# A decoder layer on one core: filler steps with later due times, and another order in the input projection

## The chip, the cores and the metric

The kernel runs on one core of a Trainium2 chip. The metric is the time of one execution on the device, in microseconds (us); lower is better. Five engines work side by side, each through its own list of instructions in order: PE (TensorE, matmuls), DVE (VectorE), ACT (ScalarE), POOL (GpSimd) and SP (SyncE, which here only starts transfers). POOL also starts transfers. PE writes its results to eight banks of PSUM, each [128, 512] in float32.

## The reference

One layer on x of [2048, 1024] in float32: a mixer and an MLP, each between two RMS norms, with residual sums.

```python
h = rms_norm(x, mix_norm_pre)
z = h @ w_in                      # [2048, 2560]: q, k, v (512 each), xr, gr (512 each)
q, k, v, xr, gr = split(z)
attn = dilated_attention(q, k, v) # 8 heads of 64; three windows (128, 1), (512, 4), (2048, 16), mixed
                                  # by their softmax denominators
xr = causal_depthwise_conv(xr)    # 4 taps
rec = rg_lru(xr) * gelu(gr)       # gated linear recurrence along the sequence
x = x + rms_norm(concat(attn, rec) @ w_out, mix_norm_post)
h = rms_norm(x, mlp_norm_pre)
x = x + rms_norm(relu(h @ w_ff_in) ** 2 @ w_ff_out, mlp_norm_post)
```

## The kernel before

**Numbers.** Each float32 operand of a large matmul is split in a high and a low part (`split`, L54: ACT writes the high part, DVE or POOL the low one, L56 and L57), and a product is three matmuls: high by high, high by low, low by high. A tile has 512 columns.

**Stages.** The sequence is cut in two halves (hf 0 and 1) of 1024 rows, each of two blocks of 512. The input projection, the recurrences of both halves and the attention of the first half come first; then for half 0 the output projection (`OutProj`, lines 867 to 869) and the first MLP product (`mlp_in`, L1082 to 1084); then the second MLP product of half 0 (`mlp_out`, L1232 to 1234) with the attention of half 1 amid it; then the same three stages for half 1, without attention.

**Input projection** (`Project`). `product` (L200) makes one tile of 512 columns with 24 matmuls: 8 k-tiles of 128 rows by three. `qkv(hf, pr)` (L211) is a pair of attention heads: six products (q, k, v for two blocks), each with its weights loaded in two halves of 256 KB and split, its result scaled (L235, L238), split and stored in DRAM. Attention of that pair loads it from there. `recurrent(hf, c)` (L299) is a pair of column tiles, 12 + c and 16 + c: four products, then conv, gates and scan, which are long chains on DVE, ACT and POOL (lines 313 to 355). The order is written as text (L2165 to 2167): "q01" is pair 1 of half 0, "r02" recurrent tile 2 of half 0, "a0" the attention of pair 0, "x2" the load of block 2. `run` (L2036) goes through it; after each q or r it loads the next one's first weights ahead. `ORDER` runs with the first attention's buffers, `BETWEEN` behind it, and `LATER` behind the loads of w_out; from there on the low parts of the projection are DVE's instead of POOL's (`pj.lo`, L2066). Behind each step of LATER five steps of `early_factors` (factors of the first two pairs of MLP weights) are written, and what is left of them at the end.

**The start.** r00 and r01 come before this order, in a stretch of its own (L2008 to 2024). `load_start` loads x of block 0 k-tile by k-tile and, at the k-tiles that `START` (L1457) names, pieces of the weights of tile 12: k-tiles 0 to 1, 2 to 3, 4 to 7. `load_w` then loads the weights of tiles 16 and 13, in two halves each. `load_next` (L154) fixes the order of issue of these loads as written.

**Second attention and filler.** `interleave` (L1397) writes the 48 units of the second attention (scores, masked softmax, transposes, values) and between them steps of `mlp_out`, its generator `rest`. One step is three matmuls of 512 columns into one of four banks, with one cast on ACT or one subtraction on DVE for a later step, and now and then loads. `fill(n)` takes n steps. A group of 16 pairs by four banks has 64 steps, and there are seven groups. What is left behind the attention comes between the loads of w_out for half 1 (L2142 to 2150), and the join of the last pair of heads ends there. Then the first two tiles of half 1's mix columns are loaded and split (`mix_columns`, L832), for the output projection.

**The planner.** What is written is not the order in which engines work. `Plan.run` (L1555) takes all instructions in the order of writing, finds what each depends on by its data and buffers, and lets `Machine` (L1645) play them through with planned costs. Each PE instruction gets a due time: the sum of the planned costs of all PE instructions written before it. Any other instruction is due before the earliest that needs it, by 0.6 of its own planned time, and at most `LAG` (70 us) behind the clock of the place where it is written. Whenever an engine is free in this play, it takes the instruction with the earliest due time of those that are ready (`issue`, L1780). So an instruction with a later due time gives way to all that are ready and due earlier, but is taken when nothing else is ready. Loads that are due more than `WINDOW` (90 us) ahead wait. The order that comes out is fixed on every engine by dependencies. On the chip each engine keeps to it and waits where the play was wrong.

Of the kernel before, what the change touches and what calls it, by code (L numbers as in the profile page):

```python
# [88 lines left out]
class Project:  # L89
# [26 lines left out]

    def load_start(self, ct, px):

        nc, p = self.nc, px
        hi = p.tile([P, KT, P], F32R, tag="wH", bufs=4, name=f"wH0_{ct}")  # L120
        lo = p.tile([P, KT, P], F32R, tag="wL", bufs=4, name=f"wL0_{ct}")
        raws = [p.tile([P, KT // 2, P], F32, tag="wraw", bufs=6, name=f"wraw0_{ct}_{i}") for i in range(2)]
        jobs = list(START)

        def weights(k):
            while jobs and jobs[0][0] <= k:
                _, k0, k1 = jobs.pop(0)
                raw = raws[k0 // (KT // 2)][:, k0 % (KT // 2):k0 % (KT // 2) + k1 - k0, :]
                self.load_next(raw, self.w_in[ct, :, k0:k1, :], px)
                split(nc, hi[:, k0:k1, :], lo[:, k0:k1, :], raw)  # L130

        self.load_x(0, px, weights)
        return hi, lo

# [1261 lines left out]

def interleave(units, rest):  # L1397

# [4 lines left out]
    def fill(n, then=None):  # L1403
        for i in range(n):
            next(rest, None)
            if i == 0 and then:
                then()
        if ends and next(ends[0], True):
            ends.pop(0)
# [40 lines left out]

FIRSTFILL = 32
LEAD = 4
EARLY7 = 10
NJ = FT // 2
KH = KT // 2
ORDER2 = (1, 6, 5, 3, 2, 7, 4), (1, 2, 6, 7, 5, 4, 3)
START = ((0, 0, 2), (1, 2, 4), (3, 4, 8))  # L1457

# [14 lines left out]
class Plan:  # L1473


    def __init__(self, tc):
        self.tc, self.nc, self.pools, self.behind = tc, tc.nc, [], []
        self.home, self.slots, self.range, self.tags = {}, {}, {}, collections.defaultdict(set)

    @contextlib.contextmanager  # L1480
# [12 lines left out]
    @contextlib.contextmanager  # L1493
    def issue_after(self, ins):
        traced = self.nc.cur_bb.bb.instructions
        n = len(traced)
        yield
        self.behind += [(i.name, ins.name) for i in self.nc.cur_bb.bb.instructions[n:] if i.engine == ins.engine]

    def places(self):  # L1500
# [54 lines left out]
    def run(self):  # L1555
# [49 lines left out]
        for rec in self.pools:  # L1605
# [7 lines left out]
            for tag in self.tags[id(rec)]:  # L1613
                for k, t in self.taken[tag][:self.slots[tag]]:
                    b0, b1 = self.range[t]
                    for (c0, c1), u in was:
                        if c0 < b1 and b0 < c1:
                            first[k] |= held[u]
        order = Machine(ins, eng, acc, first, issued, self.taken, self.slots, held, guards).run()
        info = mybir.DependencyInfo(mybir.DependencyClass.NoSync, mybir.DependencyReason.DATA)  # L1620
# [24 lines left out]
class Machine:  # L1645


    def __init__(self, ins, eng, acc, first, issued, taken, slots, held, guards):
        n = len(ins)
# [24 lines left out]
        for k in range(n):  # L1674
            clock.append(end)
            if eng[k] == "PE":
# [262 lines left out]
def trunk(tc, x, xT, g1, g2, g3, g4, w_in, conv_w, conv_b, w_r, b_r, w_i, b_i, lam, w_out, w1, w2,  # L1939
# [11 lines left out]
    with (  # L1951
# [49 lines left out]
        with contextlib.ExitStack() as st:  # L2001
# [6 lines left out]
            with sb("x0", "right") as px:  # L2008
                w = {12: pj.load_start(12, px)}
                z = pj.product(0, 12, w[12], 0, "B")  # L2010
                w[16] = pj.load_w(0, 16, nc.vector, px)
                w[13] = pj.load_w(0, 13, nc.vector, px)
# [115 lines left out]
        with per, tc.manual_schedule(engines={mybir.EngineType.PE}):  # L2128
            end = half(0, wo, ready)
            with sb("y0", "left") as pl, sb("z0", "left") as p:  # L2130
# [5 lines left out]
                with sb("at1", "right") as pa:  # L2136
                    with tc.manual_schedule(engines={mybir.EngineType.Activation, mybir.EngineType.DVE, mybir.EngineType.SP}):
                        last = interleave(attention(tc, pa, lambda k, n: bank(place[k][1], n), cst, scr, 1, mask_a, mask_b, p,
                                             sh.px, sh.px, first), rest)
# [24 lines left out]
SH = 2  # L2164
ORDER = "q00 r02 q01 a0 r03 q02 a1 q03 x2 a2 q10 a3"  # L2165
BETWEEN = "r10 r11 q11 r12 r13"
LATER = "q12 q13"

# [55 lines left out]
```

## Time and profile before

| | us |
|---|---|
| three runs, median | 2199.87 |
| the three | 2197.38, 2199.87, 2203.62 |
| the profiled execution | 2202.12 |
| its span, first to last instruction | 2200.3 |
| DVE, ACT, POOL busy of the span | 1535.4, 1235.7, 467.0 |

The profile is of one execution. Its lines give an engine, the line of the kernel and the tiles (written <- read), the count and the time. "A <- B" in a list of waits is the engine and line that stood idle, and what ended that; three numbers behind it are us in total, times, and the longest. In the chain of waits from the last instruction back to the first, the span is covered by what was waited for at each step. An engine that is idle and not waited for costs nothing. Matmuls overlap: one of 512 columns lasts about 400 ns in the rows, but the next starts much earlier, so the distance of starts is what counts. Buffer numbers are left out of the tiles' names: "z" is any result of the input projection, "o" of the second MLP product, "m" of the output projection, "S" and "SB" scores, "pT" and "pT_B" transposes, "oA" and "oB" values.

### The profile page before, as it was taken

The numbers are of one execution on the slowest core, as the hardware profiler recorded it, in microseconds if no ns is written. First come the engines' busy times: TensorE is split into PE (matmuls) and PEld (weight loads), VectorE is DVE, ScalarE is ACT, GpSimd is POOL, SyncE is SP. The second block draws the span as 40 slices with busy tenths as digits, with TensorE's granted clock in tenths as the row PEclk, the third lists the DMA queues.
The fourth block names the chain that finished last, engine by engine and source line by source line (L and its number), as shares of the span: only waits on it lengthen the run. The fifth ranks groups of instructions, "written<-read, shape, count | busy, mean of one in ns | idle before, by whom it ended". The sixth has DMA issues, their size and how long they took to land.

```text
span 2200.3 us, 30893 instructions
## 1 busy us (share of the span) xinstructions
PE 2146.3 (98%) x10264; PEld 1765.9 (80%) x10264; DVE 1535.4 (70%) x2900; ACT 1235.7 (56%) x2487; POOL 467.0 (21%) x546
## 2 busy tenths in 40 slices
PE   8999999999999999999999999989999999999998
PEld 6778878877888788887788888767878888888887
DVE  6858666878768777775677778777766565664556
ACT  6746656635444655554666668653365555654442
POOL 4652534376323001010011111013200000000003
PEclk9999999999999999999999999999999999999999
DMA  7574686355965667779677777686644434866665
GB/s 255 148 230 150 186 255 191 115 185 186 349 213 179 243 253 294 279 271 364 222 213 230 223 242 224 199 245 208 213 156 158 149 129 154 327 209 195 192 192 182
DMA packets 224116, 473.51 MB, mean 215 GB/s; under 512 B 23428, under 2 KB 78756, under 8 KB 217684
## 3 DMA queue, kind: packets, MB, share of 16 engines
q1 hardware_dynamic: 195140, 337.52, 47.8%
q0 software_dynamic: 28816, 134.01, 16.8%
q8 instruction: 81, 1.33, 0.2%
q14 instruction: 79, 0.65, 0.1%
HBM read 337.09 MB, written 151.13 MB: 222 GB/s over the span
## 4 chain that ended last, share of the span: by engine, by line
PE 81%; DVE 7%; ACT 3%; DMA 3%; POOL 2%; issue 2%; SPq 0%; DVEq 0%; POOLq 0%; ACTq 0%
PE o L1232 9%; PE o L1233 8%; PE o L1234 8%; PE za L1083 5%; PE za L1084 5%; PE za L1082 5%; PE z L207 4%; PE z L206 4%; PE z L208 4%; PE m L869 3%; PE m L868 3%; PE m L867 3%; PE zc L1082 2%; PE zc L1083 2%; PE zc L1084 2%
## 5 line engine op out<-in xcount | busy, mean ns | idle before, releaser
L206 PE MATMUL z<-hH,wH 128*128 128x512 f32 x640 | 256.8, 402 | 6.4 <-ACT wH L56 5.2
L208 PE MATMUL z<-hH,wL 128*128 128x512 f32 x640 | 258.1, 404 | 0.0
L207 PE MATMUL z<-hL,wH 128*128 128x512 f32 x640 | 257.0, 402 | 0.0
L206 PEld LDWEIGHTS z<-hH,wH 128*128 128x128 f32 x640 | 121.7, 190 | 36.8 <-ACT wH L56 5.2
L207 PEld LDWEIGHTS z<-hL,wH 128*128 128x128 f32 x640 | 121.5, 190 | 29.3 <-issue 3.4
L208 PEld LDWEIGHTS z<-hH,wL 128*128 128x128 f32 x640 | 121.6, 190 | 27.6 <-issue 4.6
L57 POOL TENSOR_TENSOR wL<-wraw,wH 128x512 fp32r<-128x512 f32 x64 | 88.0, 1386 | 68.2 <-ACT wH L56 67.7
L1087 ACT ACTIVATE sq<-sq 128x512 f32<-128x512 f32 x93 | 58.8, 632 | 71.7 <-DVE sq L1091 71.7
L1147 POOL DMA_DIRECT2D sa<-sq x31 | 16.5, 533 | 376.8 <-ACT sq L1088 371.1
L430 ACT ACTIVATE smB<-smB,stB 128x128 f32<-128x128 f32 (+3 forms) x128 | 71.5, 560 | 42.2 <-DVE stB L424 41.8
L430 ACT ACTIVATE sm<-sm,stA 128x256 f32<-128x256 f32 (+1 forms) x128 | 63.5, 498 | 48.4 <-DVE stA L424 47.4
L56 ACT CAST wH<-wraw 128x512 fp32r<-128x512 f32 (+1 forms) x81 | 47.3, 611 | 64.4 <-PE z L207 44.8
L1088 ACT ACTIVATE sq<-sq 128x512 f32<-128x512 f32 x124 | 76.9, 630 | 2.6
L57 DVE TENSOR_TENSOR tlB<-pT_B,thB 128x384 fp32r<-128x384 f32 x96 | 57.0, 597 | 29.5 <-ACT thB L56 26.5
L424 DVE CUSTOM_DVE_ANT_0 smB<-SB,mask_b 128x128 f32<-128x128 f32 (+3 forms) x128 | 59.7, 484 | 23.8 <-PE pT_B L403 14.1
L1266 POOL TENSOR_TENSOR y<-y,g4b 128x512 f32<-128x512 f32 x8 | 12.5, 1578 | 257.1 <-ACT junk_y L86 257.1
L424 DVE CUSTOM_DVE_ANT_0 sm<-S,mask_a 128x256 f32<-128x256 f32 (+1 forms) x128 | 47.8, 409 | 24.9 <-PE S L567 23.3
L56 ACT CAST thB<-pT_B 128x384 fp32r<-128x384 f32 x96 | 48.8, 513 | 24.1 <-PE pT_B L403 18.5
L238 DVE TENSOR_TENSOR zn<-z,bc 128x512 f32<-128x512 f32 x32 | 21.9, 685 | 54.1 <-PE z L208 50.0
L403 PE MATMUL pT_B<-ident,smB 128*128 128x128 f32 x320 | 54.4, 278 | 3.7 <-DVE tlA L57 1.7
L320 DVE SCALAR_TENSOR_TENSOR xc<-xr,cw,xc 128x512 f32<-128x512 f32 x48 | 51.4, 1077 | 5.9 <-POOL xc L317 5.8
L869 PE MATMUL m<-woH,m_4L 128*128 128x512 f32 x128 | 50.6, 397 | 3.4 <-DVE m_4L L57 3.4
(607 smaller groups left out, 7079.2 us busy)
## 6 DMA issues: line engine op xcount, KB each, us to landing
sa<-as POOLq DMA_DIRECT2D x31, 1024.0 KB, 6.7
w1r<-in_dram SPq DMA_DIRECT2D x56, 512.0 KB, 3.6
sa<-sq POOLq DMA_DIRECT2D x31, 768.0 KB, 4.2
wraw<-in_dram SPq DMA_DIRECT2D x79, 256.0 KB, 3.0
place<-in_dram SPq DMA_DIRECT2D x14, 1024.0 KB, 6.6
sb<-place POOLq DMA_DIRECT2D x14, 1024.0 KB, 4.2
kh<-sk SPq DMA_DIRECT2D x24, 512.0 KB, 5.6
kl<-sk SPq DMA_DIRECT2D x24, 512.0 KB, 6.8
```

The source lines that it names most:

```text
L57: (lo_eng or nc.vector).tensor_tensor(out=lo, in0=src, in1=f32(hi), op=ALU.subtract))
L206: pe.matmul(z, hi[:, k, :], hh, start=(k == 0), stop=False)
L207: pe.matmul(z, hi[:, k, :], hl, start=False, stop=False)
L208: pe.matmul(z, lo[:, k, :], hh, start=False, stop=(k == KT - 1))
L430: s.activation(out=sm[:, c0:c0 + w], in_=sm[:, c0:c0 + w], func=AF.Exp, scale=-1.0, bias=st[:, 0, u, cols[j]:cols[j] + 1], accum_out=st[:, ...
L869: pe.matmul(o, ml, wh[:, ds], start=False, stop=(k == order[-1]))
L1082: pe.matmul(o, hi[:, k], bh[:, k], start=start and k == 0, stop=False, skip_group_check=True)
L1083: pe.matmul(o, hi[:, k], bl[:, k], start=False, stop=False, skip_group_check=True)
L1084: pe.matmul(o, lo[:, k], bh[:, k], start=False, stop=k == KH - 1, skip_group_check=True)
L1232: pe.matmul(o, ah[:, ts], bh, start=fresh and j == 0, stop=False, skip_group_check=True)
L1233: pe.matmul(o, ah[:, ts], bl, start=False, stop=False, skip_group_check=True)
L1234: pe.matmul(o, al[:, ts], bh, start=False, stop=j == NJ - 1, skip_group_check=True)
```

## The change

Three things change, none in what is computed. First, `load_start` takes two column tiles, 12 and 16, and loads their weights in turns between the k-tiles of x, in four pieces of two k-tiles each. Second, the order: q01 comes first and q00 in its place, and q13 stands between r10 and r11 instead of last. Third, each step of `mlp_out` that `interleave` takes is written through `Plan.later`, which notes its instructions with 30 us; `Machine` adds that to their clock. The steps of `mlp_out` behind the attention are not noted.

```diff
-    def load_start(self, ct, px):
+    def load_start(self, cts, px):
 
-        nc, p = self.nc, px
-        hi = p.tile([P, KT, P], F32R, tag="wH", bufs=4, name=f"wH0_{ct}")
-        lo = p.tile([P, KT, P], F32R, tag="wL", bufs=4, name=f"wL0_{ct}")
-        raws = [p.tile([P, KT // 2, P], F32, tag="wraw", bufs=6, name=f"wraw0_{ct}_{i}") for i in range(2)]
+        p, made = px, {}
+        for ct in cts:
+            made[ct] = [p.tile([P, KT, P], F32R, tag=f"w{x}", bufs=4, name=f"w{x}0_{ct}") for x in "HL"]
+        raws = {ct: [p.tile([P, KT // 2, P], F32, tag="wraw", bufs=6, name=f"wraw0_{ct}_{i}") for i in range(2)] for ct in cts}
         jobs = list(START)
 
         def weights(k):
             while jobs and jobs[0][0] <= k:
                 _, k0, k1 = jobs.pop(0)
-                raw = raws[k0 // (KT // 2)][:, k0 % (KT // 2):k0 % (KT // 2) + k1 - k0, :]
-                self.load_next(raw, self.w_in[ct, :, k0:k1, :], px)
-                split(nc, hi[:, k0:k1, :], lo[:, k0:k1, :], raw)
+                for ct in cts:
+                    raw = raws[ct][k0 // (KT // 2)][:, k0 % (KT // 2):k0 % (KT // 2) + k1 - k0, :]
+                    self.load_next(raw, self.w_in[ct, :, k0:k1, :], px)
+                    hi, lo = made[ct]
+                    split(self.nc, hi[:, k0:k1, :], lo[:, k0:k1, :], raw)
 
         self.load_x(0, px, weights)
-        return hi, lo
+        return made
...
     def fill(n, then=None):
         for i in range(n):
-            next(rest, None)
+            tc.later(rest, FILLER)
...
+FILLER = 30.0
...
-START = ((0, 0, 2), (1, 2, 4), (3, 4, 8))
+START = ((0, 0, 2), (1, 2, 4), (3, 4, 6), (5, 6, 8))
...
+    def later(self, step, time):
+
+        n = len(self.nc.cur_bb.bb.instructions)
+        more = next(step, None)
+        self.shift.update((i.name, time) for i in self.nc.cur_bb.bb.instructions[n:])
+        return more
...
         for k in range(n):
-            clock.append(end)
+            clock.append(end + shift.get(ins[k].name, 0.0))
...
-                w = {12: pj.load_start(12, px)}
+                w = pj.load_start((12, 16), px)
                 z = pj.product(0, 12, w[12], 0, "B")
-                w[16] = pj.load_w(0, 16, nc.vector, px)
                 w[13] = pj.load_w(0, 13, nc.vector, px)
...
-ORDER = "q00 r02 q01 a0 r03 q02 a1 q03 x2 a2 q10 a3"
-BETWEEN = "r10 r11 q11 r12 r13"
-LATER = "q12 q13"
+ORDER = "q01 r02 q00 a0 r03 q02 a1 q03 x2 a2 q10 a3"
+BETWEEN = "r10 q13 r11 q11 r12 r13"
+LATER = "q12"
```

More of the change, by code (lines that the diff above doesn't have):

```diff
@@ L1392, in mlp_out, with interleave @@
                     pass
-def interleave(units, rest):
+def interleave(tc, units, rest):
     ends = []
@@ L1478, in __init__ @@
         self.home, self.slots, self.range, self.tags = {}, {}, {}, collections.defaultdict(set)
+        self.shift = {}
     @contextlib.contextmanager
@@ L1618, in run @@
                             first[k] |= held[u]
-        order = Machine(ins, eng, acc, first, issued, self.taken, self.slots, held, guards).run()
+        order = Machine(ins, eng, acc, first, issued, self.taken, self.slots, held, guards, self.shift).run()
         info = mybir.DependencyInfo(mybir.DependencyClass.NoSync, mybir.DependencyReason.DATA)
@@ L1645, with __init__ @@
 class Machine:
-    def __init__(self, ins, eng, acc, first, issued, taken, slots, held, guards):
+    def __init__(self, ins, eng, acc, first, issued, taken, slots, held, guards, shift):
         n = len(ins)
@@ L2137, in trunk @@
                     with tc.manual_schedule(engines={mybir.EngineType.Activation, mybir.EngineType.DVE, mybir.EngineType.SP}):
-                        last = interleave(attention(tc, pa, lambda k, n: bank(place[k][1], n), cst, scr, 1, mask_a, mask_b, p,
+                        last = interleave(tc, attention(tc, pa, lambda k, n: bank(place[k][1], n), cst, scr, 1, mask_a, mask_b, p,
                                              sh.px, sh.px, first), rest)
```

## The prediction

> **What bounds the kernel now.** The page comes first, for the engine that sets the end: its row of busy time and the chain that ended last.
>
> ```profile
> PE 2146.3 (98%) x10264; PEld 1765.9 (80%) x10264; DVE 1535.4 (70%) x2900; ACT 1235.7 (56%) x2487; POOL 467.0 (21%) x546
> ```
> ```profile
> PE 81%; DVE 7%; ACT 3%; DMA 3%; POOL 2%; issue 2%; SPq 0%; DVEq 0%; POOLq 0%; ACTq 0%
> ```
>
> PE is busy for 2146.3 of 2200.3 us, so 54.0 us are idle. The change adds and removes no matmul; it can only win idle time, or time in which matmuls run slower than their best. So the next view is the busy time by stage (columns: length, then PE, PEld, DVE, ACT, POOL busy with counts, granted clock, DMA share, GB/s).
>
> ```profile
> 0.00:20.00 20.00, 14.55 (x35) 8.73 (x36) 10.10 (x21) 11.68 (x19) 7.67 (x17) 1.00 0.87 280
> 40.00:60.00 20.00, 18.49 (x76) 13.34 (x75) 17.80 (x44) 10.70 (x18) 10.67 (x13) 1.00 0.32 108
> 60.00:80.00 20.00, 16.85 (x71) 12.71 (x70) 19.91 (x31) 17.46 (x29) 8.87 (x11) 1.00 0.46 145
> 300.00:420.00 120.00, 114.07 (x699) 96.31 (x698) 91.73 (x244) 80.77 (x220) 44.42 (x37) 0.99 0.52 166
> 420.00:560.00 140.00, 133.91 (x553) 103.05 (x552) 116.19 (x135) 66.60 (x95) 98.67 (x110) 0.99 0.61 207
> 560.00:700.00 140.00, 140.00 (x651) 116.25 (x650) 98.81 (x200) 64.09 (x146) 40.61 (x43) 1.00 0.69 237
> 1030.00:1100.00 70.00, 64.78 (x335) 52.74 (x334) 39.59 (x92) 39.72 (x94) 0.00 (x0) 1.00 0.76 254
> 1340.00:1440.00 100.00, 96.75 (x529) 80.83 (x529) 80.48 (x186) 73.81 (x153) 12.15 (x20) 0.98 0.66 198
> 1440.00:1500.00 60.00, 51.14 (x212) 40.22 (x211) 43.11 (x77) 30.76 (x58) 15.41 (x20) 0.97 0.81 239
> 1660.00:2190.00 530.00, 530.00 (x2337) 438.54 (x2337) 313.48 (x494) 273.02 (x478) 32.90 (x38) 1.00 0.57 193
> ```
>
> The last row gives the price of a matmul of 512 columns when nothing is in its way: 530 / 2337 = 0.227 us. The other rows hold the idle time in reach: 5.45 us at the start, 4.66 us from 40 to 80, 6.1 us from 420 to 560, 5.2 us where the second attention begins, 8.9 us where it ends. Who is waited for there, in the last three of these:
>
> ```profile
> PE pr L323 <- DVE xc L320: 2.5, 2, 1.4
> PE vt L250 <- DVE zn L238: 2.5, 1, 2.5
> PE z L206 <- DVE zn L235: 0.9, 1, 0.9
> ```
> ```profile
> PE SB L624 <- DVE stB L424: 2.6, 5, 1.0
> ```
> ```profile
> PE m L869 <- DVE m_4L L57: 3.4, 1, 3.4
> PE o L1232 <- ACT b_10H L1317: 2.9, 1, 2.9
> PE m L867 <- ACT m_4H L56: 1.2, 1, 1.2
> ```
>
> The first fence is 420 to 560, where all waits are for DVE; the second is the first row of 1030 to 1100; the third is 1440 to 1500, where output projection and the MLP output wait for operands.
>
> **First weights in turns.** The start in order of time, PE and then the DMA queue of SP:
>
> ```profile
> 14.26 0.63 PE L206 MATMUL z<-hH,wH 128*128 128x512 f32 x1
> 14.69 0.63 PE L207 MATMUL z<-hL,wH 128*128 128x512 f32 x1
> ```
> ```profile
> 17.70 0.39 PE L206 MATMUL z<-hH,wH 128*128 128x512 f32 x1
> 17.92 0.39 PE L207 MATMUL z<-hL,wH 128*128 128x512 f32 x1
> ```
> ```profile
> 4.49 2.52 SPq L157 DMA_DIRECT2D xr<-in_dram  x4
> 7.06 3.72 SPq L157 DMA_DIRECT2D wraw<-in_dram  x4
> ```
>
> Until about 16.9 us the first product (24 matmuls) follows the arrival of x, at 0.43 us a matmul even where they stand back to back; then they take 0.22 us. The second product (column tile 16) starts only behind it. The change puts its 0.5 MB ahead of the last x tiles: w16 goes from two loads behind x to four among it, and w12 from three loads to four, so SP issues three more DMAs, at 2.52 / 4 = 0.63 us each, and every later load queues behind them. Two products can then use each x tile: 5.4 us of PE work (24 x 0.227) move into waiting time. Against that stand 0.5 MB at the 280 GB/s of the first row, 1.9 us, and 1.9 us of issue, which overlap. PE is ahead by 5.4 - 1.9 = 3.5 us after both products, an estimate. But then comes this wait (0 to 100 us):
>
> ```profile
> PE pr L323 <- DVE xc L320: 1.9, 1, 1.9
> ```
>
> From 60 to 80 us DVE is busy for 19.91 of 20 us, and DVE's chain starts with the norm's x tiles, which come no earlier. So most of the lead becomes longer waits. I take **-1.5 us**; ends: -5 (5.4 less a little issue) and +2 (1.9 us later x, nothing won).
>
> [...]
>
> **Other order of pairs, first half.** With q01 first and q00 last, the first attention's scores need what the product just before them stored. Its price is the way through DRAM:
>
> ```profile
> kh<-sk SPq DMA_DIRECT2D x24, 512.0 KB, 5.6
> kl<-sk SPq DMA_DIRECT2D x24, 512.0 KB, 6.8
> ```
> ```profile
> sk<-zh SPq DMA_DIRECT2D x32, 128.0 KB, 3.0
> ```
>
> (Columns: queue, count, size of one, median us from issue to landing.) Store and load are 3.0 + 6.8 = 9.8 us, and the values follow later. On PE r03's four products hide it (4 x 5.4 = 21.7 us) and q02's behind them; on SP the dependent loads stand ahead of later weights and can hold them up. With the cover I cost it at **0**; if DVE is the limit there, as for the 6 us idle from 300 to 420, up to +6. Moves in the order also can win 2.
>
> **Second half: q13 between r10 and r11.** In 420 to 560 PE runs r10, r11, q11, r12, r13: DVE 116.2 of 140 us. A q pair is 24 x 6 = 144 matmuls, 32.7 us of PE, with 10 elementwise steps on DVE; a recurrent pair keeps DVE busy nearly as long as PE. Putting q13 among them gives PE something to run, so the 5.9 us of the three waits should halve: -3. On the other side q13 now comes ahead of the line that moves its low parts from POOL to DVE. In the groups of that stage and a later one:
>
> ```profile
> L320 DVE SCALAR_TENSOR_TENSOR xc<-xr,cw,xc 128x512 f32<-128x512 f32 x21 | 28.4, 1354 | 3.1 <-POOL xc L317 3.0
> L57 POOL TENSOR_TENSOR wL<-wraw,wH 128x512 fp32r<-128x512 f32 x20 | 27.6, 1386 | 7.4 <-ACT wH L56 7.3
> ```
> ```profile
> L57 DVE TENSOR_TENSOR wL<-wraw,wH x6: 678/684/693, 567.8 to 602.1; 128x512 fp32r<-128x512 f32 x6
> ```
> ```profile
> L320 DVE SCALAR_TENSOR_TENSOR xc<-xr,cw,xc 128x512 f32<-128x512 f32 x48 | 51.4, 1077 | 5.9 <-POOL xc L317 5.8
> ```
>
> Ten such steps leave DVE (6 halves of weights, 4 of q and k): 10 x 0.684 = 6.8 us less there, 10 x 1.386 = 13.9 us more on POOL. Whether POOL's work slows DVE is not settled by these rows, but L320 takes 1354 ns here and 1077 ns over the whole run. Behind q13 only q12 (32.7 us of PE) remains as cover for the early factors and w_out; the stage 560 to 700 has no idle PE and 98.8 of 140 us of DVE, so I cost that at nothing; without the cover it is what 7 us of DVE are. I take **-3 us**; ends -6 and +7.
>
> [...]
>
> **MLP output's steps due 30 us later.** They are filler amid the second attention. By the tile o, in the attention and behind it:
>
> ```profile
> 1435.20:1476.70 41.50, 37.26 (x159) 29.34 (x159) 1.09 (x2) 0.00 (x0) 1.00 0.90 272
> 1036.70:1435.20 398.50, 290.57 (x1091) 195.97 (x1091) 5.28 (x8) 9.09 (x16) 1.00 0.74 226
> ```
>
> Filler is 1091 x 0.227 = 247.7 of 398.5 us, 62%. With fillers due 30 us of planned PE time later, attention runs 30 us ahead in the list, so 0.62 x 30 = 18.6 us of filler remain for behind its last matmul, which comes about 18.6 us earlier. At its end the join of the last pair then gets its stores and loads done under filler. What is late now:
>
> ```profile
> 1467.42 0.37 SPq L839 DMA_DIRECT2D m_4L<-smix  x1
> ```
> ```profile
> 1466.49 4.27 ACT L56 CAST woH<-woL 128x512 fp32r<-128x512 f32 x8
> 1476.33 1.06 ACT L86 ACTIVATE junk_y<-y 128x1024 bf16<-128x1024 f32 x1 [5.57 <-DVE y L1242]
> ```
> ```profile
> 1482.96 0.60 ACT L56 CAST m_4H<-m_4L 128x512 fp32r<-128x512 f32 x1
> ```
>
> The planner expected the mix columns late, and put their cast behind the sums of y, though ACT stood idle for 5.57 us before. With the load 18 us earlier, 3.4 + 1.2 us go. The 2.9 us for b_10H come from a transfer amid w_out's and the join's loads; the latter move ahead of it. The fillers' own loads are due later too, but tied in a chain and to the steps that use them. So -7.5; ends -9 and 0. At the beginning attention takes its lead: PE then takes scores as soon as the plan calls them ready, as from 1030 to 1100, where 5.22 of 70 us (7.5%) are lost. For half that stretch more: 35 x 0.075 = +2.6; ends 0 and +12 (160 us). Together **-5 us**. No wait is added by hand; only orders change, on all five queues.
>
> **Sum.** -1.5 + 0 - 3 - 5 = -9.5 us. The profiled execution took 2202.1 us (span 2200.3), so 2192.6; it lies 2.25 us above the median, and against that the forecast is **2190.4 us**.
>
> **Rivals.** (a) *Everything wins* (-4.8, -6, -10): about 2179; for it speaks that each wait named is covered by work at hand, against it DVE's 19.91 of 20 us. (b) *DVE is the bound and POOL's splits hold it up*: the start wins nothing and q13 costs 7.1 us (13.9 - 6.8): 2190.4 + 1.5 + 3 + 7.1 = 2202.0. For: L320's 1354 ns; against: POOL's idle 7.4 us before wL. (c) *The shift doesn't do what it says*: keys and values arrive when due, and attention can't go ahead; the last term is nothing: 2195.4. For: DMA share 0.76 from 1030 to 1100. (d) *Slower*: attention takes all its time to gain its lead, and PE waits for DVE at each score as from 1030 to 1100: 335 us x 0.075 = 25 in place of 2.6: 2212.9. It makes the kernel slower from about 250 us of such a stretch (18.7 us); against it speaks that DVE stands at 39.6 of 70 us there, so it isn't short of time, only late.
>
> **Numbers.** About 0.3% (6.6 us) can be told from no change. Forecast 0.42, (a) 0.12, (b) 0.14, (c) 0.15, (d) 0.17. Faster: 0.42 + 0.12 = 0.54; within: 0.14 + 0.15 = 0.29; slower 0.17. The range goes from 2178, near (a), to 2207, which leaves out most of (d) and a little below, under 2 in 10.
>
> **What would show it.** At the start: w16's matmuls among w12's before 17 us, and waits for xc at 60 to 80 as long or longer. Between 420 and 600: the waits for DVE halved, L320 no longer than 1354 ns. In attention: its last pst about 18 us earlier relative to the first m, over 200 matmuls of o between them, no wait for m_4L; from 1030 to 1150 idle PE under 9 us. Wrong: more idle PE in the attention than the end wins, or new waits for keys in the first attention.

## The result, and the profile after

The changed kernel takes **2175.01 us**, the median of four runs (2173.16 to 2175.86). The kernel before took 2201.74 us, the median of the four beside it (2197.38 to 2206.09). The ratio is 0.9877, with a 95% interval of 0.9855 to 0.9900: 26.7 us less, where 9.5 were forecast. The sign was right, and the time lies below the range of 2178 to 2207 us. Three executions of the kernels further down took 6111 to 9812 us (the one of them that was profiled has 11 to 15 matmuls in each 10 us from 1430 to 1600 us), and the ratios leave these out.

The page of the changed kernel, in its row of busy time and its chain that ended last:

```profile
PE 2136.3 (98%) x10264; PEld 1754.5 (81%) x10264; DVE 1520.6 (70%) x2893; ACT 1229.1 (57%) x2486; POOL 482.5 (22%) x556
...
PE 84%; DVE 6%; ACT 5%; issue 2%; POOL 2%; DMA 1%; DVEq 0%; POOLq 0%; ACTq 0%; SPq 0%
```

The span is 2172.6 us. PE's idle time fell from 54.0 to 36.3 us, 17.7 less. But PE's busy time also fell, by 10.0 us, for the same 10264 matmuls. So there are two things to explain: waits that went, and matmuls that got faster. The stages of the prediction once more (columns as there; lines of the changed kernel stand two higher from L131 to L1451):

```profile
60.00:80.00 20.00, 18.75 (x76) 13.82 (x75) 18.51 (x27) 15.58 (x26) 11.63 (x10) 1.00 0.42 138
...
420.00:560.00 140.00, 134.45 (x574) 105.07 (x572) 100.02 (x118) 60.10 (x90) 101.35 (x107) 1.00 0.74 244
560.00:700.00 140.00, 138.48 (x636) 113.90 (x637) 106.32 (x210) 68.17 (x149) 46.37 (x49) 1.00 0.60 197
1030.00:1100.00 70.00, 68.79 (x389) 57.54 (x390) 50.28 (x115) 50.00 (x120) 5.11 (x9) 1.00 0.77 232
...
1440.00:1500.00 60.00, 60.00 (x274) 49.81 (x273) 47.26 (x105) 33.55 (x78) 19.09 (x19) 1.00 0.79 235
```

The two ends of the second attention have changed most. The 70 us from 1030 on had 5.22 us of idle PE and have 1.21, with 389 matmuls in place of 335. The attention now begins earlier, though; counted over 64 us from its own first S (1036.7 us before, 1004.9 after), it is 5.22 and 1.92. In the 60 us behind 1440 there is no idle time left, and 274 matmuls run where 212 did. The stretch with q13, 420 to 560, still has 5.55 us. To place the 27.7 us that the span lost, I take the starts of each stage's first matmul from the two traces:

| stage | before, us | after, us | difference |
|---|---|---|---|
| start to first m of half 0 (projection, first attention) | 610.94 | 602.59 | -8.35 |
| to the first o of half 0 | 403.99 | 402.38 | -1.61 |
| to the first m of half 1 (second MLP product, second attention) | 461.85 | 451.16 | -10.69 |
| to the last m of half 1 (output projection) | 99.06 | 92.26 | -6.80 |
| to the last o | 617.42 | 617.29 | -0.13 |

So 17.5 us lie in the two stages that the shift acts on, and 8.35 in the projection. The 1.61 are no part's: they are one dip of the clock, at 734 us, which the next lines show.

**Where the matmuls got faster.** Here is the kernel before in pieces of 10 us; the third number from the right is the granted clock:

```profile
310.00:320.00 10.00, 7.31 (x47) 7.17 (x48) 8.09 (x29) 6.50 (x23) 4.47 (x5) 0.83 1.02 346
490.00:500.00 10.00, 9.13 (x35) 7.45 (x36) 3.62 (x7) 0.59 (x1) 1.34 (x2) 0.83 0.83 316
730.00:740.00 10.00, 8.21 (x28) 6.00 (x28) 10.00 (x18) 6.30 (x13) 0.00 (x0) 0.83 0.28 85
1400.00:1410.00 10.00, 10.00 (x49) 8.39 (x48) 6.68 (x15) 5.95 (x13) 0.00 (x0) 0.85 0.65 212
1480.00:1490.00 10.00, 5.38 (x19) 3.83 (x18) 9.21 (x19) 4.57 (x11) 5.20 (x4) 0.91 0.62 153
1490.00:1500.00 10.00, 10.00 (x42) 8.17 (x42) 4.31 (x9) 2.59 (x7) 3.98 (x4) 0.92 0.61 178
1600.00:1610.00 10.00, 6.95 (x23) 4.95 (x22) 10.00 (x17) 7.95 (x15) 0.00 (x0) 0.83 0.24 77
```

These are all pieces below 0.95 ahead of the last 10 us. Seen closer, behind the wait of 3.4 us for m_4L:

```profile
1488.00:1490.00 2.00, 1.75 (x4) 1.47 (x5) 1.54 (x3) 0.00 (x0) 0.46 (x1) 0.56 0.92 222
1490.00:1492.00 2.00, 2.00 (x7) 1.53 (x7) 0.00 (x0) 0.00 (x0) 0.00 (x0) 0.58 0.93 362
1492.00:1494.00 2.00, 2.00 (x10) 1.69 (x9) 0.31 (x2) 0.69 (x2) 0.00 (x0) 1.00 1.11 248
```

From 1488.3 to 1491.6 us the granted clock is 0.50, and a matmul starts every 0.43 us instead of every 0.227. The other rows show the same: 0.50 over 3.3 us from 314.1, 491.6, 734.0, 1399.6 and 1604.4 us on. A mean of 0.83 over 10 us is 0.50 for 3.4 us of them, and costs 1.7 us (0.17 of 10 us). The kernel before has six such dips, 10.2 us. The changed kernel has one:

```profile
1570.00:1580.00 10.00, 6.95 (x23) 5.03 (x23) 10.00 (x18) 8.97 (x17) 0.00 (x0) 0.83 0.34 112
```

Five dips fewer are 8.5 of the 10.0 us by which PE is less busy. The waits ahead of the dips are no longer than 3.4 us, and mostly shorter. Not each wait brings a dip: the 2.9 us for b_10H at 1459 us did not (the granted clock is 1.00 from 1457 to 1470 us), a wait of 2.1 us at 1396 us did (0.50 from 1399.6 us on). Two waits of 1.0 and 0.8 us, at 732 and 733 us, had one behind them, and the changed kernel has the same two at 723 and 724 us without one (1.00 from 720 to 735 us). So that dip went by chance, and what decides is not shown.

### The profile page after: what moved, and what is told of

The parts are those of the page before. It is cut to its first block, busy times and chain, and to the rows that moved or that the text cites. A ratio compares the mean times of both kernels' runs of the same rounds, so it can differ in the third digit from the quotient of the medians.

```text
span 2172.6 us, 30852 instructions
## 1 busy us (share of the span) xinstructions
PE 2136.3 (98%) x10264; PEld 1754.5 (81%) x10264; DVE 1520.6 (70%) x2893; ACT 1229.1 (57%) x2486; POOL 482.5 (22%) x556
## 4 chain that ended last, share of the span: by engine, by line
PE 84%; DVE 6%; ACT 5%; issue 2%; POOL 2%; DMA 1%; DVEq 0%; POOLq 0%; ACTq 0%; SPq 0%
PE o L1234 9%; PE o L1236 9%; PE o L1235 9%; PE za L1085 5%; PE za L1086 5%; PE za L1084 5%; PE z L210 4%; PE z L209 4%; PE z L208 4%; PE m L871 3%; PE m L870 3%; PE m L869 3%; PE zc L1084 3%; PE zc L1085 3%; PE zc L1086 3%; PE oB L652 2%
## 5 line engine op out<-in xcount | busy, mean ns | idle before, releaser
L57 POOL TENSOR_TENSOR wL<-wraw,wH 128x512 fp32r<-128x512 f32 x70 | 96.0, 1384 | 55.9 <-ACT wH L56 54.4
L1268 POOL TENSOR_TENSOR y<-y,g4b 128x512 f32<-128x512 f32 x8 | 12.4, 1573 | 257.1 <-ACT junk_y L86 257.1
L426 DVE CUSTOM_DVE_ANT_0 sm<-S,mask_a 128x256 f32<-128x256 f32 (+1 forms) x128 | 47.5, 408 | 23.4 <-PE S L569 23.3
L405 PE MATMUL pT_B<-ident,smB 128*128 128x128 f32 x320 | 59.9, 277 | 1.7 <-DVE tlB L57 0.9
L57 POOL TENSOR_TENSOR zl<-zn,zh 128x512 fp32r<-128x512 f32 x28 | 39.4, 1408 | 61.9 <-ACT zh L56 52.5
```

Source lines behind the costliest of these rows:

```text
L57: (lo_eng or nc.vector).tensor_tensor(out=lo, in0=src, in1=f32(hi), op=ALU.subtract))
L426: v.tensor_tensor_reduce(out=sm[:, c0:c0 + w], in0=sp[:, c0:c0 + w], in1=mask[:, mask.shape[-1] - w:], scale=1.0, scalar=3.0e38, op0=ALU.a ...
```

## The experiments

"Before" is always the kernel before, run beside each. Ratios have 95% intervals.

**Each part alone.** Four kernels, each the kernel before with one part of the change: the shift (`FILLER = 30.0`), the first weights in turns (`load_start((12, 16), px)` with the new `START`), the swap in `ORDER`, and q13's move.

```diff
-ORDER = "q00 r02 q01 a0 r03 q02 a1 q03 x2 a2 q10 a3"
+ORDER = "q01 r02 q00 a0 r03 q02 a1 q03 x2 a2 q10 a3"
```
```diff
-BETWEEN = "r10 r11 q11 r12 r13"
-LATER = "q12 q13"
+BETWEEN = "r10 q13 r11 q11 r12 r13"
+LATER = "q12"
```

> The kernel before with the later due times of the filler alone (30 us). Theory A, each part acts in its own stage and the parts add up: all that the changed kernel won between the first o of half 0 and the last m of half 1, 10.7 + 6.8 = 17.5 us, comes from this part, so about 2184 us (2181 to 2188), and the first m of half 0 stays where it was (610.9 us in the span). Rival B, the planner plays everything through anew and the gain is that of one lucky order: the part alone gives something else, under 9 us or over 25 us.

> The kernel before with the first weights in turns alone. Theory A: PE's lead of about 4 us at the twelfth product of the input projection is kept to the end: about 2198 us. Rival, as the prediction had it: DVE is the bound from 40 to 80 us and takes most of it back: 2200 us or more. Rival B: the order further on changes too and gives or takes several us.

> The kernel before with q01 ahead of q00 alone. Theory A: nothing, 2202 us within 2, since the way of q00 through DRAM lies behind r03's products. Rival: the first attention waits for its keys, up to 6 us slower; or the order by itself wins some of the 4 us that the changed kernel has by then.

> The kernel before with q13 between r10 and r11 alone. Theory A: what is left of the 8.3 us up to the first m of half 0 when 4 us are the start's: 4 us, about 2198 us, with the waits of PE for DVE from 420 to 600 us down. Rival: POOL's splits hold DVE up, 2202 us or more, with more than 6 us of such waits.

| alone | median, us | ratio | us by the ratio | forecast |
|---|---|---|---|---|
| shift | 2184.02 | 0.9916 [0.9890, 0.9942] | -18.5 | -5 |
| turns | 2197.11 | 0.9987 [0.9967, 1.0006] | -2.9 | -1.5 |
| swap | 2195.71 | 0.9978 [0.9961, 0.9995] | -4.8 | 0 |
| q13 | 2203.03 | 1.0008 [0.9993, 1.0022] | +1.8 | -3 |

The kernel before took 2201.96 us beside them. The parts add up to -24.4 us, near the whole's 26.7, but the intervals of the turns and of q13 include no change at all. The shift's term is off by 13.5 us, the other three by 1 to 5 each. So the shift is taken apart first.

**Where the shift wins.** The 48 units of the second attention are cut in two: the shift is given only to the steps written with units 0 to 23, or only to those with 24 to 47 (`at[0]` is the unit that is being written).

```diff
-            tc.later(rest, FILLER)
+            tc.later(rest, FILLER if at[0] < 24 else 0.0)
```

(The other kernel has `at[0] >= 24`.)

> The kernel before, with the 30 us shift of the MLP's steps only for those issued with the first 24 of the second attention's 48 units; the steps beside the last 24 stand where they stood. Theory A (the shift wins in two separate places, and each follows from which half of the steps is shifted): the first S of half 1 stands as early as with the whole shift (no o matmul before it), PE's idle time at 1030 to 1100 us falls from 5.2 to below 2 us, but the lead is given back by the middle, some 159 o matmuls are left after the last pst as before, and PE still waits for m_4L and b_10H. Time: 4 us less than the kernel before, 0.998. Rival B (the beginning only moves its waits further back; all of the gain belongs to the end): the same time as before within 1 us, with the idle time at 1100 to 1400 us larger by what 1030 to 1100 loses. Rival C (a lead once taken is kept): about 250 o matmuls after the last pst and the whole gain, 0.9915.

> The kernel before, with the 30 us shift of the MLP's steps only for those issued with the last 24 of the second attention's 48 units. Theory A: the beginning stays as before (96 o matmuls before the first S of half 1, 5.2 us of idle time at 1030 to 1100 us), the end is that of the whole shift: about 250 o matmuls after the last pst, no wait for m_4L, m_4H and b_10H, no idle time of PE at 1440 to 1500 us, and the output projection's mean matmul at its fast value. Time: 12 us less than the kernel before, 0.9945. Rival B (all of the gain belongs to the end): 0.9915. Rival C (only the named waits of 7.5 us go, and the matmuls of the output projection are no faster): 0.9965.

> The kernel with the shift for the first 24 units alone, once more, for a profile (in the profiled execution before, TensorE's matmuls took 1.1 us each throughout). Theory A: TensorE's idle time at 1036 to 1100 us below 2 us in place of 5.2, about 355 matmuls there in place of 308, with idle time at 1440 to 1500 us as in the kernel before (8.9 us). Rival B (the beginning only moves its waits): the idle time at 1100 to 1400 us grows by 3 us.

The first kernel was measured twice, the second time for another profile: 0.9987 [0.9973, 1.0002] and 0.9978 [0.9960, 0.9996]. The second half alone gave 0.9972 [0.9959, 0.9985]. The busy time by stretch, in this order: before, shift for the first half (second run), for the last half, for all:

```profile
1036.00:1100.00 64.00, 58.78 (x308) 47.75 (x308) 39.59 (x92) 39.72 (x94) 0.00 (x0) 1.00 0.73 243
1440.00:1500.00 60.00, 51.14 (x212) 40.22 (x211) 43.11 (x77) 30.76 (x58) 15.41 (x20) 0.97 0.81 239
```
```profile
1036.00:1100.00 64.00, 62.80 (x360) 52.85 (x361) 45.65 (x104) 45.89 (x112) 5.12 (x9) 1.00 0.81 245
1440.00:1500.00 60.00, 51.97 (x207) 41.30 (x206) 42.89 (x82) 30.19 (x63) 13.62 (x16) 0.91 0.78 225
```
```profile
1036.00:1100.00 64.00, 58.80 (x304) 47.65 (x303) 36.25 (x86) 36.50 (x88) 0.00 (x0) 1.00 0.77 252
1440.00:1500.00 60.00, 58.60 (x257) 47.60 (x256) 47.47 (x92) 37.84 (x73) 12.83 (x13) 1.00 0.94 290
```
```profile
1036.00:1100.00 64.00, 62.65 (x357) 52.41 (x358) 46.55 (x111) 46.26 (x113) 5.14 (x9) 1.00 0.81 245
1440.00:1500.00 60.00, 60.00 (x270) 49.71 (x270) 48.20 (x97) 37.98 (x79) 15.85 (x16) 1.00 0.90 280
```

Each half of the shift moves its own row and leaves the other as it was: theory A. In the kernel before, 96 o matmuls stand ahead of the first S of half 1, and then the first units run with too few of them between. With the shift none stands ahead, and the same units find filler: over 64 us from the first S on the idle time is 1.94 us in place of 5.22, so the beginning wins 3.3 us where the prediction had it lose 2.6. (The window of the rows starts 25 us later in that attention and shows 4.0.) With the first half alone the stage from the first o to the first m of half 1 is 3.1 us shorter, and the output projection behind it no faster (99.5 us). With the last half alone the output projection takes 92.3 us, as with the whole shift. Against the expected 0.9945, though, this half won half as much, and a new wait stands where the shift sets in. The longest wait of PE from 1250 to 1440 us there:

```profile
PE S L567 <- DVE stA L424: 3.6, 1, 3.6
```

The chain of waits goes back to a load of b_14L that took 7.8 us, with DVE's subtraction on it ahead of stA. The whole shift has no wait of that size there. A dip of the clock follows it (0.83 from 1280 to 1290, 1.7 us).

By the ratios the whole is more than its halves (-18.5 against -3 to -5 and -6), but the difference is about as large as the intervals are together. In the two stages that the shift acts on it is small: in the profiles the halves win 2.6 and 7.6 us there, the whole 12.4, and the new wait with its dip is more than what is missing. Ahead of these stages the executions differ by themselves: up to the first m of half 0 the orders of PE, DVE, ACT and POOL are the same in all these kernels, and yet that m comes at 609.6 us with the whole shift, at 607.6 and 614.9 with the halves, and at 610.9 in the kernel before. So it isn't shown that the whole is more than its halves.

**How large a shift.** The kernel before with `FILLER = 10.0` and with `FILLER = 60.0`.

> The kernel before with a shift of 10 us in place of 30 and nothing else; in its order 52 o matmuls stand before the first S of half 1 (96 without a shift, none with 30 us) and 189 after the last pst (159 and 249). Theory A (each o matmul kept back covers waits in proportion, at both ends): about a third of the end's 12 us and half of the beginning's 4, 6 us less than the kernel before, 0.9973. Rival B (the end's waits are chains of fixed length, of which the later ones need the last of the 249): only the beginning's 2 us and less than 2 at the end, 0.9985. Rival C (the first few o matmuls are enough): most of the whole shift's gain, 0.994 or below.

> The kernel before with a shift of 60 us in place of 30 and nothing else; in its order no o matmul stands before the first S of half 1, as with 30 us, and 331 stand after the last pst (249). Theory A (a certain cover ends the waits; with 30 us only 5.7 us of idle time are left at 1000 to 1500 us, and 1.6 of them in the first S): as with 30 us, 0.9916, no more than 2 us off. Rival B (82 o matmuls fewer, 18 us of fill, starve the attention, whose units wait for VectorE as at 1036 to 1100 us in the kernel before): 4 us more than with 30 us, 0.9935. Rival C (the gain goes on with the shift): 0.989 or below.

With 10 us the ratio is 0.9991 [0.9976, 1.0005], with 60 it is 0.9958 [0.9937, 0.9979]; with 30 it was 0.9916. So the gain isn't in proportion. With 10 us rival B came out by its time. With 60 us the stage from the first o of half 0 to the first m of half 1 is 4.3 us longer in the profile than with 30 (460.5 and 456.3): the size of its rival B, but behind the last pst and not where the attention begins. The other 5.3 us between these two profiles lie ahead of the first m of half 0, where PE's order is the same. With 10 us:

```profile
1036.00:1100.00 64.00, 61.05 (x332) 50.47 (x331) 39.96 (x101) 41.32 (x102) 0.00 (x0) 1.00 0.82 261
1440.00:1500.00 60.00, 52.88 (x213) 41.17 (x213) 44.36 (x82) 32.40 (x63) 12.63 (x16) 0.94 0.86 252
```

The beginning wins its half, the end almost nothing. The reason is the place of one cast in ACT's order. The groups of tile m_4L from 1430 to 1500 us before, and from 1390 after (duration of one, minimum, median, maximum in ns, then first and last start):

```profile
L839 SPq DMA_DIRECT2D m_4L<-smix x4: 371/414/703, 1467.4 to 1494.7; - x4
...
L57 DVE TENSOR_TENSOR m_4L<-m_4L,m_4H x1: 1747/1747/1747, 1486.4 to 1486.4; 128x512 fp32r<-128x512 f32 x1
```
```profile
L841 SPq DMA_DIRECT2D m_4L<-smix x6: 359/374/543, 1441.3 to 1490.0; - x6
...
L57 DVE TENSOR_TENSOR m_4L<-m_4L,m_4H x1: 681/681/681, 1450.2 to 1450.2; 128x512 fp32r<-128x512 f32 x1
```

The last pst starts at 1435.07 before and at 1397.70 after, so the operand that the output projection waits for is done 53.1 and 53.2 us behind it (1488.1 and 1450.9). It is no sooner; PE comes to it later, 61.7 us behind the last pst in place of 49.7, since 249 o matmuls are left in place of 159. But rival B's reason, chains of fixed length, doesn't hold. With 10 us 189 are left, PE comes at 57.2, and the operand is done only at 59.4. With 60 us it is done at 84.4, and PE comes at 91.2. With 10 us ACT, and then after the change:

```profile
1475.91 1.06 ACT L86 ACTIVATE junk_y<-y 128x1024 bf16<-128x1024 f32 x1 [5.80 <-DVE y L1242]
1482.54 0.60 ACT L56 CAST m_4H<-m_4L 128x512 fp32r<-128x512 f32 x1
```
```profile
1449.33 0.61 ACT L56 CAST m_4H<-m_4L 128x512 fp32r<-128x512 f32 x1
1455.02 1.06 ACT L86 ACTIVATE junk_y<-y 128x1024 bf16<-128x1024 f32 x1 [4.03 <-DVE y L1244]
```

With 10 us m_4L's loads have landed by 1472.1 us, but the cast stands behind the four sums of y, and these wait for the last o matmuls of their group. So o matmuls that are kept back push the cast back too: it starts 5.5 us behind the first m of half 1, and 6.2 us behind it in the kernel before, where the prediction had found it at 1482.96. In the changed kernel it stands ahead of the sums and starts 6.8 us ahead of the first m, with 60 us 5.2. In the profiles the wait for m_4L is there wherever the cast stands behind the sums, and gone wherever it stands ahead of them. So the end is won when the planner turns this order around, somewhere between 10 and 30 us; where was not tried. With 60 us the filler is late itself; PE's waits from 1250 to 1440 us:

```profile
PE o L1233 <- DVE b_14L L1319: 4.2, 1, 4.2
PE o L1232 <- ACT b_11H L1317: 1.3, 1, 1.3
```

**The start.** Two kernels ask what the turns win. One leaves the loads as before but makes the small DVE chain for the decay constants (tile sp, 26 operations) due at the very start; the other has the turns, and holds this chain back until behind the first convolution.

```diff
-            pj.recurrent_consts(conv_w, conv_b, w_r, b_r, w_i, b_i, lam)
+            with tc.due(-130.0):
+                pj.recurrent_consts(conv_w, conv_b, w_r, b_r, w_i, b_i, lam)
```
```diff
+        if (hf, c, b) == (0, 0, 0):
+            self.decay(conv.ins)
```

(`due` notes a time for all that is written in it, as `later` does; `decay` is the chain, taken out of `recurrent_consts` and issued behind `conv`.)

> The kernel before, with only the constants of the recurrence (the two bias rows and the small chain of 26 VectorE operations on tile sp) due so early that they stand between the first splits, ahead of the reciprocal of the first norm; the first weights are loaded as before. Theory A (what the turns win at the start is that this chain leaves the stretch at 44 to 62 us, in which VectorE has no idle time): the chain's 6.0 us are gone from 40 to 80 us, the first 768 matmuls of the z product end 4 us earlier, and the time is that of the turns alone, 0.998 (4 us less). Rival B (what wins is TensorE's earlier start on the second weight tile): 1.000, within 1 us, since TensorE's first 20 us are unchanged. Rival C (the two share it): 2 us less.

> The kernel with the first weights in turns and nothing else, with the chain of 26 small VectorE operations on tile sp held back until after the convolution of block 0's first channels, so that it stands in the stretch at 44 to 62 us again as in the kernel before. Theory A (the chain's place is the gain): the time is that of the kernel before, 1.000, within 1 us. Rival B (TensorE's earlier start on the second weight tile is the gain): the time of the turns alone, 0.998. Rival C (the two share it): half of it, 0.999.

The first gave 1.0006 [0.9991, 1.0020], the second 0.9997 [0.9983, 1.0011]. Where the chain runs, as DVE's busy time on tile sp, in the kernel before and in that with the turns alone:

```profile
40.00:60.00 20.00, 5.54 (x22) 1.00 0.32 108
```
```profile
20.00:40.00 20.00, 2.89 (x18) 1.00 0.98 362
```

The chain moves out of DVE's fullest stretch as a consequence of the turns, though no line of the change names it. Of PE's waits from 50 to 80 us the kernel before has the 1.9 us for xc and this one, the chain's end; the changed kernel has neither:

```profile
PE pr L323 <- DVE ncs L289: 1.3, 1, 1.3
```
```profile
PE pr L325 <- ACT r L330: 1.2, 1, 1.2
PE pbc L197 <- DVE dg L196: 0.3, 1, 0.3
```

After 192 matmuls of the projection, at 66.50 us before, the turns alone are 3.0 us ahead, with the chain held back 1.35 us, and the chain early without turns 0.5 us (there it also holds up a low part of the first weights, a wait of 2.8 us). So neither is enough: the lead of PE is worth 1.35 there, and the chain's place 1.7 more once PE has the lead. The final times differ by less than their intervals, so this is read from the traces only; by time neither theory is decided.

**The swap.** At 312 us the kernel before waits 3.4 us for stA, and the swap has no such wait. DVE and POOL in the kernel before around it, in order of time (start, duration):

```profile
304.56 6.84 DVE L181 SCALAR_TENSOR_TENSOR hL<-xr,g_sb,hH 128x512 fp32r<-128x512 f32 x2 [1.58 <-ACT hH L180]
```
```profile
305.85 2.54 POOL L57 TENSOR_TENSOR wL<-wraw,wH 128x512 fp32r<-128x512 f32 x2
308.34 1.28 POOL L57 TENSOR_TENSOR zl<-zn,zh 128x512 fp32r<-128x512 f32 x1
309.58 1.26 POOL L728 TENSOR_TENSOR na<-na,co 128x512 f32<-128x512 f32 x1
```

Two operations that take 0.75 us each elsewhere take 6.84. The second began at 305.43 and ended at 311.40, half a us behind POOL's row of four. In the kernel with the swap alone POOL's row there is two operations long, and hL stands behind DVE's stA:

```profile
308.87 2.69 DVE L181 SCALAR_TENSOR_TENSOR hL<-xr,g_sb,hH 128x512 fp32r<-128x512 f32 x1
```

The next experiment takes the first two operations of that row away from POOL, in the kernel before:

```diff
-        self.ahead[hf, ct] = self.load_w(hf, ct)
+        self.ahead[hf, ct] = self.load_w(hf, ct, self.nc.vector if (hf, ct) == (1, 0) else None)
```

> The kernel before, with the two low parts of q10's first weights (two operations of 128x512) made by VectorE where GpSimd makes them; these two begin GpSimd's row of four to five operations without a gap at 305.85 to 310.84 us, beneath which VectorE's hL of the third token block lasts 5.97 us in place of 0.75, and TensorE waits 3.4 us (to 5.3 in other profiles) for stA behind it. Theory A (VectorE's hL is held until GpSimd's row ends, and that is the stall which the swap of q01 and q00 removes): without these two the hL is done within 3 us, TensorE's idle time at 305 to 320 us falls below 1 us, and the time is that of the swap alone, 0.998 (3 to 5 us less). Rival B (the stall belongs to late loads of the third block, whatever GpSimd does): the stall stays at 3 us or more and the time at 1.000. Rival C (the wait moves to the next GpSimd row): the stall goes, but 320 to 430 us take it back, 1.000.

The wait shrank as theory A has it:

```profile
PE S L567 <- DVE stA L424: 0.9, 1, 0.9
```

But the kernel got slower, 1.0047 [1.0032, 1.0061]: after 3.2 us won by 425 us it lost 8 by the end of the projection, with a wait of 4.4 us at 539 where the planner's order now came out otherwise. That is rival C, and worse. So what holds DVE up at 305 us is shown. That the swap's 4.8 us are this wait and its dip (3.4 and 1.7) fits, but isn't shown by itself. In the profiles the wait goes with the order: of ten kernels with q00 first and POOL's row untouched nine have it, at 3.4 to 5.3 us, and of the five with q01 first none has. The wait also varies between executions of one order: with q13's move alone, whose order is the same up to some 410 us, POOL's row began later and the wait was absent.

**q13 and the low parts.** Three kernels on the changed one: q13 put back behind q12; the low parts of half 1's weights that are loaded ahead made by DVE (`self.nc.vector if hf else None` in the line above); and both.

> The changed kernel with q13 back behind q12, so with the first weights in turns, the swap of q01 and q00 and the shift. Theory A (q13's move is worth nothing: VectorE's operations are held by GpSimd for 37 us at 400 to 600 us in either order, only elsewhere): 0.988 of the kernel before, as the changed kernel, within 1.5 us of it. Rival B (in company of the other parts the move wins the 3 us that were forecast): 0.9895. Rival C (the move costs, as its 1.0008 alone leaves open): 0.986.

> The changed kernel with the low parts of all weights of half 1 that are loaded ahead made by VectorE in place of GpSimd. Theory A (VectorE's time at 400 to 600 us goes into operations held by GpSimd's rows, and TensorE's 7 us of waits there follow from it): GpSimd's rows get shorter, VectorE is held for less than 25 us in place of 37, TensorE's waits at 420 to 620 us fall below 4 us, 3 to 4 us less than the changed kernel, 0.9865 of the kernel before. Rival B (VectorE's own work is the bound: 0.68 us more for each low part): the same or longer, 0.988 to 0.990.

> The changed kernel with q13 back behind q12 and with the low parts of half 1's weights that are loaded ahead made by VectorE. Theory A (what GpSimd holds up at 400 to 600 us costs TensorE little that isn't found again elsewhere): within 2 us of the changed kernel, 0.988 of the kernel before. Rival B (the two add up: 1 us by q13 and 2 to 3 by the low parts): 0.9865.

The ratios are 0.9890 [0.9869, 0.9910], 0.9894 [0.9869, 0.9919] and 0.9893 [0.9871, 0.9914], medians 2173.61, 2173.98 and 2175.26 us: all the same as the changed kernel. For each DVE operation from 400 to 600 us that lasts over 0.4 us longer than the fastest tenth of its kind, I add up the excess: 36.9 us before, 37.4 with q13's move alone, 36.5 in the changed kernel, 30.0 with q13 back, 23.3 with the low parts on DVE, 28.0 with both. All of these operations overlap with some of POOL's. PE's waits from 420 to 620 us in the changed kernel, then with the low parts on DVE (the three longest):

```profile
PE pr L325 <- DVE xc L322: 3.6, 4, 1.2
PE z L208 <- DVE gr L347: 2.0, 2, 1.7
PE vt L252 <- DVE zn L240: 1.4, 1, 1.4
```
```profile
PE z L208 <- DVE state L344: 1.7, 1, 1.7
PE pr L325 <- DVE vs L57: 1.3, 1, 1.3
PE pr L325 <- DVE xc L322: 0.8, 1, 0.8
```

Thirteen us less of held DVE moved the waits and took 1.6 us from their sum (7.0 to 5.4), and the time didn't change measurably. Theory A is right for DVE, and not for the time.

## Why the prediction was right or wrong

**What bounds the kernel** was right: PE, with idle time in the stages named. It was also said that matmuls slower than their best could be won, and then no term priced them. That is the first gap: a wait can have a price of 1.7 us behind it, and 8.5 of the 27.7 us are that (1.7 of them, at 734 us, by luck).

**The shift (-5 forecast; -18.5 alone by the ratio, 12.4 in its own two stages of the profile, 17.5 there in the changed kernel)** is the step that failed: the beginning had the wrong sign, and the dips of the clock behind the waits were put at nothing.
- *The end, -7.5.* The mechanism held: 249 o matmuls behind the last pst (over 200 forecast), the cast of m_4H ahead of the sums of y, no wait for m_4L, m_4H or b_10H, the last pst about 17 us further from the first m (41.7 us before, 58.4 after). So did the size: from the last pst to 20 us behind the first m PE is idle for 1.1 us in place of 8.9. One reason was wrong: the loads of w_out and of the mix columns did not move ahead of b_10's. In both kernels six of w_out's go out between the last pst and it, ten more behind it, and the mix columns' behind it too. It lands 5.1 us behind its issue in place of 10.8; why is open.
- *The beginning, +2.6.* The sign was wrong. The 7.5% of idle time at 1030 to 1100 us were taken for the way in which attention runs when it leads. They were the way in which it runs when its filler has been spent ahead of it: with 96, 52 and no o matmuls ahead of the first S the idle time is 5.2, 2.95 and 1.9 us. So the beginning won 3.3 us (under 9 of idle time was forecast, as a growth).
- *What had no term.* Two dips of the clock, at 1400 and 1488 us, are 3.4 us. Another 2.4 us of idle time went between the two places. With that 7.8 + 3.3 + 3.4 + 2.4 = 16.9 of the 17.5 us have a place. The shift alone has neither dip, but doesn't win the 2.4 us, though PE's order is the same from the first o of half 0 to the last m of half 1: five profiles with this order are 12.4 to 17.5 us shorter there than the kernel before. So a few of the 17.5 us are luck.

**The start (-1.5)** came out at -2.9, inside its bounds; the interval includes no gain as well as the -1.5. The lead was there: w16's matmuls begin among the x tiles, and the last matmul of two products starts at 19.8 us in place of 22.9, a lead of 3.1 us where 3.5 were estimated. The spacing of the matmuls first falls from 0.43 to 0.23 us at 9.8 in place of 17.2 us; what decides when it falls is not shown. Wrong was that longer waits for xc take the lead: the wait of 1.9 us went, and it was down to 0.3 us also where the decay chain was held back in DVE's fullest stretch. What the chain's place takes away is the wait of 1.3 us for its end.

**The swap (0, ends -2 and +6)** measured -4.8, beyond its end (the interval reaches from -8.6 to -1.1). Only the way through DRAM was priced, and that was rightly covered. The stall at 312 us stood in the profile, within the 6 us from 300 to 420; who held DVE there wasn't looked up.

**q13 (-3)** measured +1.8 alone, within its noise, and nothing in company. The waits didn't halve: 7.0 us at 420 to 620 after, 5.9 before. L320's mean did fall, from 1354 to 1165 ns, but at other lines DVE was held as long as before. Rival (b), POOL's work holding DVE up, was seen at 305 us, but its price, +7.1, didn't come either. That price takes DVE as held for the whole of POOL's 13.9 us, which no run shows for q13's steps: with q13 put back in the changed kernel the excess of DVE's operations was 30.0 us in place of 36.5, and the time the same.

**The rivals.** (a), everything wins, came nearest at 2179, by its sign in each part but q13, and partly by luck: it had q13 at -6 and the shift at -10. (d), the loss from a leading attention, has no trace. (c) fell with the first S of half 1, 31.9 us earlier, 21.9 of them against the first o.

## What to carry to other kernels

Price a wait from its stage and not from its row, since behind a PE wait the clock can stay low for a while (here 0.50 for 3.4 us, 1.7 us of time, six times in the kernel before). A list that starts late on one kind of work needs the other kind kept for both ends. How much to keep is not a matter of filling time alone: look whether the operand at the end is made behind or ahead of work that waits for the filler itself. Here 249 matmuls kept back turned that order around, 189 did not, and 331 cost 4.3 us more in their stage. Before a difference of some us is put down to an edit, compare executions where the order is the same: six of them took 607.6 to 614.9 us to the first m of half 0. Small edits to a planned order move things that they don't name, so compare the orders before pricing the edit.

## What the runs showed of the hardware

**DVE behind a row of POOL's.** One DVE operation with two inputs in SBUF (hL), of 0.75 us elsewhere, took 5.97 us in the kernel before under four POOL operations that followed each other without a gap (305.85 to 310.84 us). It ended 0.56 us behind the last of them, at 311.40 us; the first was over at 307.15. With the swap alone and in the changed kernel the row is two operations long, and an hL took 2.69 us in each, to 0.56 us behind the row's end. With the shift alone a fifth POOL operation (1.25 us) followed the fourth, and the two hL that take 6.84 us in the kernel before took 8.92, again to 0.56 us behind the row's end. So in these four profiles DVE's operation ended with POOL's row, whether that had two, four or five operations. With q13's move alone, where the two began at 303.79 us and POOL's row only at 306.59, they took 2.45 us. POOL's operations are longer at times, too (1.73 us in place of 1.29 for the one at 304.48 us with the swap alone); what decides is open.

**Half clock after a wait.** Some 3.4 us at a granted clock of 0.50, 1.7 us of time, six times in the kernel before: four times behind one wait of 2.1 to 3.4 us, and behind two pairs of waits, of 1.7 and 1.3 us at 1602 us and of 1.0 and 0.8 us at 732. The changed kernel's four runs lie within 2.7 us, the four of the kernel before beside them within 8.7. That the dips make this difference isn't shown: six runs with the shift alone lie within 10.7.
